# Both MLPs of a two-layer trunk: seven block products for four more groups of the down projection, with shared buffers

## Chip, cores and metric

One core of a Trainium2 chip runs the whole kernel. The metric is the device time of one execution in microseconds; lower is better. Each group of runs is told by its median.

## The reference, cut to what matters

The input is a sequence of 1024 tokens of width 1024. A state-space layer with a gated linear unit (GLU), an MLP, a stick-breaking attention layer and a second MLP follow each other, each added to the residual stream through a gate that depends on a vector `c`. Both MLPs are

```python
h = modulate(rms_norm(x, mlp_norm_g[i]), sh_m, sc_m)
ff = einsum('bsf,fd->bsd', square(relu(einsum('bsd,df->bsf', h, mlp_w1[i]))), mlp_w2[i])
x = x + g_m[:, None, :] * ff
```

with an inner width of 4096. All of it is float32. The gates, shifts and scales (`ada_chunks`) are products of `silu(c)` with matrices of 1024 rows, and the projections of keys, values and queries have a bias that is the product of such a shift with their weights.

## The kernel before

Activations lie transposed: 128 features on the partitions, 512 tokens (a half, `h` = 0 or 1) in a row. A product of two float32 numbers is made of three float32r matmuls (`mm3`, L243): both operands are split into a rounded high part (`uh`, `hi`) and the rest (`ul`, `lo`). The high part is a copy on ScalarE (ACT), the rest a subtraction on VectorE (DVE).

**The MLP** (`mlp`, from L873) has 32 inner tiles in 8 groups `c` of four (`j` = 0 to 3). For an inner tile, `ups` loads one weight unit of 128x1024 (512 KB) into a `raw` buffer through SyncE's queue (SP), splits it, and `up` makes 24 matmuls for each half; ACT takes the relu from PSUM into a buffer `r`, DVE squares it, and `halves` splits it into two tiles of a ring `f`. The down projection of a group has 4 output pairs `op`. *Plain*: for each of 2 outputs and 2 halves, 4 inner tiles times 3 matmuls, so 192 matmuls in a group, and one DVE operation (`down`, L93 in the profile) adds the gated sum to the residual tile. *Seven products*: the 2x2 blocks (2 outputs x 2 halves) are multiplied with seven block products in place of eight, each of 6 matmuls, so 168 in a group. For this `enter` adds and subtracts the hidden blocks (right operands T1 to T4, B11, B21, B22), `blocks` adds and subtracts the weight blocks, the first three of which are split on ACT and DVE and the other four on GpSimd (POOL: four adds of 128x256, a cast and a subtraction of 128x1024), and `seven` gathers the products in two sum tiles `u` and `v`. Before the change `fast(c)` is true for groups 1 to 6 of the second MLP alone.

The order of an MLP is: `ups` of the next group's first inner tile, the down projection of this group, `ups` of the next group's other three tiles. In the last group the plain code goes through the outputs twice, once for each half, and loads each weight unit twice.

**Side work.** During the GLU stage and the first MLP, a list `side` is worked off by `pump`: `mid` takes 3 or 4 jobs after every output pair and every inner tile. Its jobs are of three kinds. A `gemv` (L171) loads 512 KB into a `raw` buffer, the same three buffers that the MLP's weights go through, and DVE multiplies and sums it against a row (`silr` for the gates and shifts, `row` for the biases). A `shift_row` brings a shift into `row` by PE and ACT. A `keep` (L221) prepares half a unit of the attention's weights on POOL: DMA into a buffer `ks`, scale, cast into `kr`, subtract, and two DMAs out (`kh`, `kl`), all issued from POOL's queue. There are 16 `keep` jobs in the GLU stage and 48 in the first MLP.

The order of instructions on each engine is set when the program is built: tiles, pools and waits come from the framework, whose scheduler orders the instructions of all engines; every engine then works in order. A tile of a pool waits until the last reader of the buffer that it takes is done.

Of the kernel before, what the change touches and what calls it, by code (L numbers as in the profile page):

```python
# [30 lines left out]
W2_COLS = (range(8), (0, 1, 2, 3, 6, 7, 4, 5))  # L31
# [25 lines left out]
def kernel(ctx, tc, A, out):  # L57
# [163 lines left out]
    def keep(key, src, c, scale=None):  # L221
# [3 lines left out]
        raw = adap.tile([P, HN], F32, tag="ks", name=nm("ks"), bufs=2)  # L225
# [32 lines left out]
    def s5(hook):  # L258
# [19 lines left out]
        def wide(tag):  # L278
            return un_tile(tag, F32)

# [578 lines left out]
    def open_f(n):  # L859
        fp = ctx_f.enter_context(tc.tile_pool(name="fp", bufs=1))  # L860

        def ft(tag, bufs, dt=F32):
            return fp.tile([P, HN], dt, tag=tag, name=nm(tag), bufs=bufs)

        def f_tile(dt=F32R):
            return ft("f", n, dt)

        return ft, f_tile

    def mlp(layer, xs, hs, norm, fs, mid=None, done=None):  # L870
        w1, w2 = A["w1"][layer], A["w2"][layer]
        gm = M_GM0 if layer == 0 else M_GM1
        ft, f_tile = fs  # L873
        hid, raws = {}, {}

        def up(f, u, h):
# [3 lines left out]
            r = ft("r", 2 + 4 * layer)  # L880
# [10 lines left out]
        def down(c, o, u, i, h):  # L891
            p = ps_ax()
            for j in range(4):
                mm3(p, u, W2_COLS[layer][4 * i + j], hid[j, h], j == 0, j == 3)
# [3 lines left out]
        def enter(j, h, r):  # L898
            raws[j, h] = r
            if h == 0 and j < 2:  # L900
                hid["B11", j] = halves(r)
            if (j, h) == (1, 1):
                for i in range(2):
                    t = ft("t", 2)
                    sub(t, raws[i, 1], raws[i, 0])
                    hid["T1", i] = halves(t)
            if h == 1 and j >= 2:
                i = j - 2
# [3 lines left out]
                sub(b12, b22, b12)  # L912
                hid["T3", i] = halves(b12)
                add(b11, b11, b12)
# [22 lines left out]
        def seven(c):  # L937
            us, sums, op_ = {}, {}, [0]
# [5 lines left out]
            def product(op, n):  # L944
# [10 lines left out]
                op_[0] = op  # L955
                if n == 1:
                    sums[op] = ft("t", 2), ft("t", 2)
                    ACT.copy(sums[op][0], p)
# [4 lines left out]
                elif n == 6:  # L963
                    add(sums[op][0], p, sums[op][0])
                elif n == 5:
                    u, v = sums[op]
                    add(v, p, u)
                    gain(0, 1, v)
                elif n == 7:
                    u, v = sums[op]  # L970
# [7 lines left out]
            for op in range(4):  # L978
                for n in (1, 2, 4, 6, 5, 7, 3):
                    product(op, n)  # L980

        def plain(c, j, h, r):
            raws[j, h] = r
            late = c == 7 and layer == 1
            if not late or h == 0 or j > 1:
                hid[j, h] = halves(r)
            elif j == 1:
                hid[0, 1], hid[1, 1] = halves(raws[0, 1]), halves(r)

        def fast(c):  # L990
            return layer == 1 and 0 < c < 7

        def ups(c, j):
            u = load_unit(w1[4 * c + j])
            for h in range(2):
                r = up(4 * c + j, u, h)
                if fast(c):
                    enter(j, h, r)
                else:
                    plain(c, j, h, r)  # L1000
# [10 lines left out]
        for c in range(8):  # L1011
            if c < 7:
                held = dict(hid)
                hid.clear()
                ups(c + 1, 0)
                nxt = dict(hid)
                hid.clear()
                hid.update(held)
                if fast(c):
                    seven(c)  # L1020
                else:
                    for op in range(4):
                        u = load_unit(w2[c, op])
                        for i in range(2):
                            for h in range(2):
                                down(c, 2 * op + i, u, i, h)
                        if mid is not None:
# [698 lines left out]
```

## Time and profile before

| | us |
|---|---|
| median of 3 runs | 2512.99 (2507.63 to 2521.70) |
| the profiled execution, its own time | 2512.54 |
| span of its profile | 2510.7 |
| TensorE (PE) busy | 2358.1 (94%) |
| VectorE (DVE) busy | 1739.4 (69%) |
| ScalarE (ACT) busy | 939.4 (37%) |
| GpSimd (POOL) busy | 882.1 (35%) |

The stages, in us from the start of the span: the state-space layer to about 250, the GLU to about 405, the first MLP to 1143, attention to about 1800, its output projection to about 1850, the second MLP to the end. PE's matmuls overlap, so that its busy time is no measure of its pace; a count of matmuls over a stretch is. The granted clock of TensorE was 0.973 of full speed over the run.

### The profile page before, as it was taken

The numbers are of one execution on the slowest core, as the hardware profiler recorded it, in microseconds if no ns is written. First come the engines' busy times: TensorE is split into PE (matmuls) and PEld (weight loads), VectorE is DVE, ScalarE is ACT, GpSimd is POOL, SyncE is SP. The second block draws the span as 40 slices with busy tenths as digits, with TensorE's granted clock in tenths as the row PEclk, the third lists the DMA queues.
The fourth block names the chain that finished last, engine by engine and source line by source line (L and its number), as shares of the span: only waits on it lengthen the run. The fifth ranks groups of instructions, "written<-read, shape, count | busy, mean of one in ns | idle before, by whom it ended". The sixth has DMA issues, their size and how long they took to land.

```text
span 2510.7 us, 33266 instructions
## 1 busy us (share of the span) xinstructions
PE 2358.1 (94%) x12560; PEld 1986.0 (79%) x12560; DVE 1739.4 (69%) x2536; ACT 939.4 (37%) x1704; POOL 882.1 (35%) x939
## 2 busy tenths in 40 slices
PE   3888999999999999999899999998999999999999
PEld 2677788878778888888788888887778888888887
DVE  7997547775567553345687878788583777877774
ACT  5753124221121221133566666676351332223221
POOL 4663460376786000013333323343110323342330
PEclk8998999999999999998999999999999999999999
DMA  4225862666767441123111122126621111111113
GB/s 150 87 78 187 297 215 101 237 229 222 248 206 270 154 139 55 51 90 116 64 55 39 64 68 68 58 88 214 246 86 59 34 51 59 59 34 59 51 67 109
DMA packets 105920, 299.18 MB, mean 119 GB/s; under 512 B 13344, under 2 KB 25632, under 8 KB 105760
## 3 DMA queue, kind: packets, MB, share of 16 engines
q1 hardware_dynamic: 87840, 242.52, 28.2%
q0 software_dynamic: 15360, 50.34, 5.7%
q10 hardware_dynamic: 2560, 4.20, 0.7%
q8 instruction: 99, 1.62, 0.3%
q14 instruction: 61, 0.50, 0.1%
HBM read 243.33 MB, written 49.48 MB: 117 GB/s over the span
## 4 chain that ended last, share of the span: by engine, by line
PE 65%; DVE 15%; DMA 10%; issue 4%; ACT 3%; POOL 1%; SPq 0%; DVEq 0%; ACTq 0%; POOLq 0%
PE pm L247 9%; PE pm L249 9%; PE pm L248 9%; PE pm L70 8%; DMA raw<-in_adaT_dram 5%; PE pa L953 3%; PE pa L952 3%; PE pa L954 3%; PE pa L247 3%; PE pa L249 3%; PE pa L248 3%; PE pt L70 3%; DVE sn L1236 3%; PE z L70 2%; PE po L70 2%
## 5 line engine op out<-in xcount | busy, mean ns | idle before, releaser
L247 PE MATMUL pm<-h,uh 128*128 128x512 f32 x1200 | 467.7, 392 | 8.7 <-ACT r L881 8.6
L249 PE MATMUL pm<-h,ul 128*128 128x512 f32 x1200 | 468.7, 392 | 3.1 <-DVE ul L84 3.1
L248 PE MATMUL pm<-h,uh 128*128 128x512 f32 x1200 | 469.5, 391 | 0.0
L214 ACT CAST uh<-raw 128x1024 fp32r<-128x1024 f32 x138 | 145.1, 1051 | 535.2 <-PE pa L248 155.1
L84 DVE TENSOR_TENSOR ul<-raw,uh 128x1024 fp32r<-128x1024 f32 (+1 forms) x162 | 202.5, 1250 | 141.2 <-ACT uh L214 109.4
L247 PEld LDWEIGHTS pm<-h,uh 128*128 128x128 f32 x1200 | 226.8, 189 | 58.7 <-ACT r L881 11.6
L249 PEld LDWEIGHTS pm<-h,ul 128*128 128x128 f32 x1200 | 226.4, 189 | 51.9 <-DVE ul L84 4.5
L248 PEld LDWEIGHTS pm<-h,uh 128*128 128x128 f32 x1200 | 226.7, 189 | 47.9 <-DVE h L93 0.9
L174 DVE CUSTOM_DVE_ANT_0 junk<-raw,silr 128x1024 bf16<-128x1024 f32 x95 | 133.2, 1402 | 142.3 <-DMA raw<-in_adaT_dram 142.2
L70 PE MATMUL pm<-uh,h 128*128 128x256 f32 x960 | 225.5, 301 | 4.1 <-POOL h L75 3.0
L1236 DVE TENSOR_TENSOR_SCAN sn<-sn 128x768 f32<-128x768 f32 (+7 forms) x128 | 180.4, 1415 | 48.8 <-ACT sn L1231 47.5
L887 ACT CAST f<-r 128x512 fp32r<-128x512 f32 x152 | 94.3, 621 | 253.7 <-DVE r L78 216.7
L247 PE MATMUL pa<-f,uh 128*128 128x512 f32 x464 | 181.9, 392 | 3.3 <-DVE xall L93 2.7
L248 PE MATMUL pa<-f,uh 128*128 128x512 f32 x464 | 181.4, 391 | 0.2 <-DVE f L84 0.2
L249 PE MATMUL pa<-f,ul 128*128 128x512 f32 x464 | 181.1, 390 | 0.0
L70 PEld LDWEIGHTS pm<-uh,h 128*128 128x128 f32 x960 | 170.2, 197 | 6.2 <-POOL h L75 3.2
L81 POOL TENSOR_TENSOR acc<-acc,sq 128x512 f32<-128x512 f32 x24 | 34.7, 1445 | 351.8 <-ACT sq L819 351.7
L84 DVE TENSOR_TENSOR f<-r,f 128x512 fp32r<-128x512 f32 x152 | 124.4, 820 | 45.2 <-ACT f L887 43.9
L81 POOL TENSOR_TENSOR raw<-raw 128x256 f32<-128x256 f32 x24 | 22.3, 931 | 377.8 <-DVE ul L84 377.8
L93 DVE SCALAR_TENSOR_TENSOR x<-pa,mod,x 128x512 f32<-128x512 f32 x143 | 103.4, 743 | 61.9 <-PE pa L249 59.8
L70 PE MATMUL pm<-ul,h 128*128 128x256 f32 x480 | 138.4, 288 | 0.0
L78 DVE TENSOR_TENSOR r<-r 128x512 f32<-128x512 f32 (+1 forms) x130 | 97.0, 746 | 57.6 <-ACT r L881 57.6
(371 smaller groups left out, 5471.0 us busy)
## 6 DMA issues: line engine op xcount, KB each, us to landing
raw<-in_w_dram SPq DMA_DIRECT2D x144, 512.0 KB, 3.3
raw<-in_adaT_dram SPq DMA_DIRECT2D x96, 512.0 KB, 4.0
uh<-kh SPq DMA_DIRECT2D x40, 512.0 KB, 4.0
ul<-kl SPq DMA_DIRECT2D x40, 512.0 KB, 4.1
kh<-kr POOLq DMA_DIRECT2D x64, 256.0 KB, 2.6
kl<-ks POOLq DMA_DIRECT2D x64, 256.0 KB, 3.7
raw<-in_wT_dram SPq DMA_DIRECT2D x24, 512.0 KB, 4.2
raw<-in_wglu_dram SPq DMA_DIRECT2D x20, 512.0 KB, 4.5
```

Of the source, the lines that this page charges most:

```text
L70: return lambda *a, **k: tc.keep_in_program_order(f(*a, **k))
L78: eng.tensor_tensor(o, a, b, op=ALU.mult)
L84: eng.tensor_tensor(o, a, b, op=ALU.subtract)
L93: V.scalar_tensor_tensor(o, a, s, b, op0=op0, op1=op1)
L174: V.tensor_tensor_reduce(junk, raw, row, 1.0, 0.0, op0=ALU.mult, op1=ALU.add, accum_out=bcol)
L214: ACT.copy(uh, raw)
L247: T.matmul(ps, uh[:, sl], hi, start=first, stop=False)
L248: T.matmul(ps, uh[:, sl], lo, start=False, stop=False)
L249: T.matmul(ps, ul[:, sl], hi, start=False, stop=last)
L887: ACT.copy(hi, r)
L952: T.matmul(p, uh[:, sl], hi, start=(i == 0), stop=False)
L1236: V.tensor_tensor_scan(g[:, s0:], g[:, s0:], g[:, s0:], 1.0, op0=ALU.mult, op1=ALU.bypass)
```

## The change

- `fast` is true for groups 4, 5 and 6 of the first MLP and for 1 to 7 of the second. The columns of `w2` are ordered in the same way for both layers.
- The hidden tiles of both MLPs are now one ring of 28 (`Inner`; before 20 and 30), which the norm's tiles share. The squares have two buffers `ra` for `j` < 2 and two `rb` for `j` >= 2 (before: 2 buffers `r` in the first MLP, 6 in the second); `u` and `v` take the two `rb` buffers. The inner tiles of a group are made in the order 0, 2, 1, 3.
- In group 7 of the second MLP all four results of an output pair are written out after it.
- To make room: `ks` has one buffer (before 2), `gemv` writes its product over `raw` in place of `junk`, and `row` is gone: `shift_row` writes over `silr`. For that the side list has all `gemv` jobs with `silr` first, then the first `shift_row` with 16 bias jobs, then the second with 8. The numbers of jobs are the same. Later pools have 3 `raw` buffers in place of 2.

```diff
-        pools["raw"] = es.enter_context(tc.tile_pool(name=f"raw{i}", bufs=3 - i))
+        pools["raw"] = es.enter_context(tc.tile_pool(name=f"raw{i}", bufs=3))
...
-        V.tensor_tensor_reduce(junk, raw, row, 1.0, 0.0, op0=ALU.mult, op1=ALU.add, accum_out=bcol)
+        V.tensor_tensor_reduce(raw, raw, row, 1.0, 0.0, op0=ALU.mult, op1=ALU.add, accum_out=bcol)
...
-        raw = adap.tile([P, HN], F32, tag="ks", name=nm("ks"), bufs=2)
+        raw = adap.tile([P, HN], F32, tag="ks", name=nm("ks"), bufs=1)
...
+    class Inner:
+        def __init__(self):
+            self.n, self.es, self.pools = 0, ExitStack(), {}
+        def open(self, name):
+            self.pools[name] = self.es.enter_context(tc.tile_pool(name="fp" + name, bufs=1))
+        def tile(self, dt=F32R):
+            a = self.n % 28 < 8
+            self.n += 1
+            return self.pools["ab"[not a]].tile([P, HN], dt, tag="f", name=nm("f"), bufs=8 if a else 20)
+        def raw(self, tag):
+            return self.pools["b"].tile([P, HN], F32, tag=tag, name=nm(tag), bufs=2)
...
-            r = ft("r", 2 + 4 * layer)
+            r = fs.raw(tag)
...
         def fast(c):
-            return layer == 1 and 0 < c < 7
+            return c in ((4, 5, 6), range(1, 8))[layer]
...
+                if c == 7:
+                    for k in range(2 * op, 2 * op + 2):
+                        for h in range(2):
+                            done(k, h)
...
+                for j in (2, 1, 3):
+                    ups(c + 1, j)
...
-    queue(ada_chunk(M_KSH) + [lambda: shift_row(M_KSH)] + bias_jobs(0, 16)
-          + ada_chunk(M_SHA1) + [lambda: shift_row(M_SHA1)] + bias_jobs(16, 24) + [kq_gain]
-          + ada_chunk(M_GA1) + ada_chunk(M_SHM1)
-          + ada_chunk(M_SCM1, lambda: scale_cols(3, M_SCM1)) + ada_chunk(M_GM1), 2,
+    queue(ada_chunk(M_KSH) + ada_chunk(M_SHA1) + ada_chunk(M_GA1) + ada_chunk(M_SHM1)
+          + ada_chunk(M_SCM1, lambda: scale_cols(3, M_SCM1)) + ada_chunk(M_GM1)
+          + [lambda: shift_row(M_KSH)] + bias_jobs(0, 16)
+          + [lambda: shift_row(M_SHA1)] + bias_jobs(16, 24) + [kq_gain], 2,
```

Three places of the built program show what this moves. The first is POOL while `keep` jobs run in the first MLP, before: the load into the second `ks` buffer (here `ks_5672`) is issued ahead of the subtraction of the first.

```order
L232 CAST kr_5589<-ks_5588 128x512
L227 DMA ks_5672<-in_wkv_dram 128x512
L84 TENSOR_TENSOR ks_5588<-ks_5588,kr_5589 128x512
L235 DMA kh_5586<-kr_5589 128x512
L235 DMA kl_5587<-ks_5588 128x512
L78 TENSOR_TENSOR ks_5672<-ks_5672,scl 128x512
```

The same engine in the changed program, where the 45th of all 64 `keep` jobs meets the first weight blocks of group 4 (`raw_6556`): the load of the next `ks` stands behind the DMA out of this one, and the blocks' cast and subtraction stand behind that load.

```order
L81 TENSOR_TENSOR raw_6556<-raw_6556 128x256
L84 TENSOR_TENSOR ks_6747<-ks_6747,kr_6748 128x512
L235 DMA kh_6745<-kr_6748 128x512
L84 TENSOR_TENSOR raw_6556<-raw_6556 128x256
L235 DMA kl_6746<-ks_6747 128x512
L84 TENSOR_TENSOR raw_6556<-raw_6556 128x256 x2
L227 DMA ks_6836<-in_wkv_dram 128x512
L947 CAST uh_6560<-raw_6556 128x1024
L78 TENSOR_TENSOR ks_6836<-ks_6836,scl 128x512
L84 TENSOR_TENSOR ul_6561<-raw_6556,uh_6560 128x1024
```

A load now waits for its predecessor's `kl`, and four more instructions of a block stand between a `keep` job's own. The third place is DVE in the down projection of group 4. Before, `gemv` jobs (the ISA rows) stand between the gated sums (`xall`):

```order
L93 SCALAR_TENSOR_TENSOR xall<-pa_6598,mod,xall 128x512
L174 ISA junk,mod<-raw_6967,silr 128x1024
L174 ISA mod 128x1
L93 SCALAR_TENSOR_TENSOR xall<-pv_6612,mod,xall 128x512
L174 ISA junk,mod<-raw_6978,silr 128x1024
L174 ISA mod 128x1
```

In the changed program the bias jobs of the first `shift_row` stand between the products' sums (`rb_6554` and `rb_6555` are `u` and `v`); there are 15 of them in this down projection, and 8 in that of group 5:

```order
L174 ISA raw_6653,bias<-raw_6653,silr 128x1024
L174 ISA bias 128x1
L174 ISA raw_6739,bias<-raw_6739,silr 128x1024
L174 ISA bias 128x1
L93 SCALAR_TENSOR_TENSOR xall<-pv_6678,mod,xall 128x512
L93 SCALAR_TENSOR_TENSOR xall<-pa_6687,mod,xall 128x512
L93 SCALAR_TENSOR_TENSOR xall<-pa_6695,mod,xall 128x512
L174 ISA raw_6742,bias<-raw_6742,silr 128x1024
L174 ISA bias 128x1
L81 TENSOR_TENSOR rb_6554<-pv_6703,rb_6554 128x512
```

The sums of a product are thus queued behind loads of 512 KB. Before, such bias jobs stood in the down projections and inner tiles of groups 1 to 3.

## Rows read from the trace of the kernel before

**Rows 1.** The page, part 1: busy us (share of the span) and instructions.

```profile
PE 2358.1 (94%) x12560; PEld 1986.0 (79%) x12560; DVE 1739.4 (69%) x2536; ACT 939.4 (37%) x1704; POOL 882.1 (35%) x939
```

**Rows 2.** Stretches: length, PE busy (count), PEld, DVE, ACT, POOL, clock, DMA, GB/s.

```profile
465.00:848.00 383.00, 365.35 (x1578) 297.66 (x1577) 247.55 (x294) 70.44 (x100) 252.51 (x286) 0.98 0.67 230
848.00:1020.00 172.00, 172.00 (x761) 142.41 (x760) 84.20 (x119) 35.45 (x50) 0.00 (x0) 1.00 0.30 101
1960.00:2440.00 480.00, 480.00 (x2119) 397.61 (x2118) 375.12 (x485) 133.39 (x199) 169.99 (x144) 1.00 0.15 52
```

**Rows 3.** Timeline of ACT: the relu before groups 0's and 4's down projections.

```profile
464.73 0.59 ACT L881 ACTIVATE r<-pm 128x512 f32<-128x512 f32 x1
...
848.11 0.59 ACT L881 ACTIVATE r<-pm 128x512 f32<-128x512 f32 x1
```

**Rows 4.** Waits of PE, 400 to 1150: total us, times, longest.

```profile
PE pm L247 <- ACT r L881: 7.6, 5, 2.6
```

**Rows 5.** Groups by shape, DVE, 600 to 810: busy us, mean ns, idle before.

```profile
L174 DVE CUSTOM_DVE_ANT_0 junk<-raw,row 128x1024 bf16<-128x1024 f32 x20 | 30.6, 1528 | 16.0 <-DMA raw<-in_wT_dram 15.3 <-ACT row L1523 0.6
...
L84 DVE TENSOR_TENSOR f<-r,f 128x512 fp32r<-128x512 f32 x16 | 17.3, 1081 | 6.2 <-ACT f L887 6.2
L78 DVE TENSOR_TENSOR r<-r 128x512 f32<-128x512 f32 x16 | 15.5, 971 | 5.8 <-ACT r L881 5.8
```

**Rows 6.** Groups by shape, DVE, 1960 to 2440.

```profile
L93 DVE SCALAR_TENSOR_TENSOR x<-pa,mod,x 128x512 f32<-128x512 f32 x96 | 68.8, 741 | 2.0
L93 DVE SCALAR_TENSOR_TENSOR x<-t,mod,x 128x512 f32<-128x512 f32 x72 | 66.5, 944 | 0.8
L81 DVE TENSOR_TENSOR t<-pa,t 128x512 f32<-128x512 f32 x96 | 63.8, 684 | 21.2 <-PE pa L954 21.1
...
L84 DVE TENSOR_TENSOR r<-r,r 128x512 f32<-128x512 f32 x24 | 31.4, 1310 | 0.4
```

**Rows 7.** Groups by shape, POOL, 468 to 810: one `keep` job's compute.

```profile
L84 POOL TENSOR_TENSOR ks<-ks,kr 128x512 f32<-128x512 f32 x48 | 67.5, 1407 | 1.5
L78 POOL TENSOR_TENSOR ks<-ks,scl 128x512 f32<-128x512 f32 x48 | 65.1, 1358 | 125.3 <-DVE scl L93 71.5 <-DMA ks<-in_wkv_dram 38.4 <-DMA ks<-in_wq_dram 14.9
L232 POOL CAST kr<-ks 128x512 fp32r<-128x512 f32 x48 | 44.9, 936 | 15.4 <-DMA kh<-kr 13.6
```

**Rows 8.** DMA issues, 600 to 720, then 840 to 960: KB, median us to landing.

```profile
raw<-in_wT_dram SPq DMA_DIRECT2D x12, 512.0 KB, 4.4
...
kl<-ks POOLq DMA_DIRECT2D x16, 256.0 KB, 3.7
...
ks<-in_wkv_dram POOLq DMA_DIRECT2D x13, 256.0 KB, 3.4
...
raw<-in_w_dram SPq DMA_DIRECT2D x13, 512.0 KB, 3.4
```

**Rows 9.** Timeline of POOL: start, us, what, idle before it and its releaser.

```profile
468.71 3.40 POOL L78 TENSOR_TENSOR ks<-ks,scl 128x512 f32<-128x512 f32 x2 [71.55 <-DVE scl L93]
...
638.89 0.54 POOL L235 DMA_DIRECT2D kl<-ks  x1
...
642.26 0.54 POOL L227 DMA_DIRECT2D ks<-in_wkv_dram  x1 [0.84 <-DMA kl<-ks]
...
646.77 1.20 POOL L78 TENSOR_TENSOR ks<-ks,scl 128x512 f32<-128x512 f32 x1 [1.64 <-DMA ks<-in_wkv_dram]
```

**Rows 10.** Groups by shape, POOL, 1960 to 2440: one `blocks` call has 1, 3, 1, 1.

```profile
L84 POOL TENSOR_TENSOR ul<-raw,uh 128x1024 fp32r<-128x1024 f32 x24 | 63.5, 2646 | 1.9
L84 POOL TENSOR_TENSOR raw<-raw 128x256 f32<-128x256 f32 x72 | 59.2, 822 | 5.6
L930 POOL CAST uh<-raw 128x1024 fp32r<-128x1024 f32 x24 | 25.0, 1041 | 29.3 <-PE pm L248 28.2
L81 POOL TENSOR_TENSOR raw<-raw 128x256 f32<-128x256 f32 x24 | 22.3, 931 | 377.8 <-DVE ul L84 377.8
```

**Rows 11.** Timeline at the end of the span: the last DVE operation.

```profile
2506.24 0.75 DVE L93 SCALAR_TENSOR_TENSOR x<-pa,mod,x 128x512 f32<-128x512 f32 x1 [1.97 <-PE pa L249]
```

More of the change, by code (lines that the diff above doesn't have):

```diff
@@ L30 @@
 LEAD = 24
-W2_COLS = (range(8), (0, 1, 2, 3, 6, 7, 4, 5))
+W2_COLS = (0, 1, 2, 3, 6, 7, 4, 5)
 NONE = 3
@@ L279, in wide @@
             return un_tile(tag, F32)
+        row = st([P, D], "row")
         braw = wide("uh").rearrange("p (l q h) -> p l q h", l=2, q=32)
@@ L872, in mlp, with up @@
         gm = M_GM0 if layer == 0 else M_GM1
-        ft, f_tile = fs
+        f_tile = fs.tile
         hid, raws = {}, {}
-        def up(f, u, h):
+        def up(f, u, h, tag="ra"):
             p = ps_mm()
@@ L899, in enter @@
             raws[j, h] = r
[L900 to L906, printed above, removed]
+            i = j % 2
+            if (j, h) == (1, 0) or (j, h) == (2, 0):
+                hid["B11", i] = halves(raws[i, 0])
             if h == 1 and j >= 2:
-                i = j - 2
                 b11, b12, b21, b22 = raws[i, 0], raws[i, 1], raws[j, 0], raws[j, 1]
@@ L937, in seven @@
         def seven(c):
-            us, sums, op_ = {}, {}, [0]
+            us, op_, uv = {}, [0], (fs.raw("rb"), fs.raw("rb"))
             def gain(i, h, src):
@@ L955, in product @@
                 op_[0] = op
+                u, v = uv
                 if n == 1:
-                    sums[op] = ft("t", 2), ft("t", 2)
-                    ACT.copy(sums[op][0], p)
+                    ACT.copy(u, p)
                 if n < 3:
@@ L963, in product @@
                 elif n == 6:
[L964 removed]
+                    add(u, p, u)
                 elif n == 5:
[L966 removed]
                     add(v, p, u)
@@ L980, in seven @@
                     product(op, n)
+                if mid is not None:
+                    mid()
+                if c == 7:
+                    for k in range(2 * op, 2 * op + 2):
+                        for h in range(2):
+                            done(k, h)
         def plain(c, j, h, r):
             raws[j, h] = r
[L984 to L988, printed above, removed]
+            if c and j == 0:
+                return
+            if c and (j, h) == (2, 0):
+                hid[0, 0], hid[0, 1] = halves(raws[0, 0]), halves(raws[0, 1])
+            hid[j, h] = halves(r)
         def fast(c):
-            return layer == 1 and 0 < c < 7
+            return c in ((4, 5, 6), range(1, 8))[layer]
         def ups(c, j):
@@ L1012, in mlp @@
             if c < 7:
-                held = dict(hid)
-                hid.clear()
                 ups(c + 1, 0)
[L1016 to L1027, printed above, removed]
-                            mid()
-                hid.clear()
-                hid.update(nxt)
-                for j in range(1, 4):
-                    ups(c + 1, j)
+            if fast(c):
+                seven(c)
+            elif c < 7:
+                for op in range(4):
+                    u = load_unit(w2[c, op])
+                    for i in range(2):
+                        for h in range(2):
+                            down(c, 2 * op + i, u, i, h)
                     if mid is not None:
@@ L1041, in mlp @@
                             done(2 * op + i, h)
+            if c < 7:
+                for j in (2, 1, 3):
+                    ups(c + 1, j)
+                    if mid is not None:
+                        mid()
     def attention(xn, bias, xd):
@@ L1444 @@
     silr = rowp.tile([P, D], F32, name="silr")
-    junk = rowp.tile([P, D], BF16, name="junk")
-    row = rowp.tile([P, D], F32, name="row")
     def gate(i):
@@ L1522, in shift_row @@
                          start=True, stop=True)
-            ACT.copy(row[:, HN * h:HN * h + HN], p)
+            ACT.copy(silr[:, HN * h:HN * h + HN], p)
     def kq_gain():
@@ L1701, in _layout @@
     a["w2"] = np.stack([w.reshape(8, 4, 128, 4, 2, 128).transpose(0, 3, 2, 4, 1, 5).reshape(8, 4, 128, 8, 128)[
-        :, :, :, list(cols)].reshape(8, 4, 128, 1024) for w, cols in zip(mlp_w2, W2_COLS)])
+        :, :, :, list(W2_COLS)].reshape(8, 4, 128, 1024) for w in mlp_w2])
     return {k: np.ascontiguousarray(v) for k, v in a.items()}
```

64 lines of the change are left out of this document (31 added, 33 removed).

## The prediction

> **What bounds the kernel now.** I read the page first, then the stretches of both MLPs, then who waits there, and last the queues that the change touches. The page has PE at 94% of the span [rows 1], but that is a mean. What is to be seen in the stretches is the count of matmuls. In the second MLP PE starts 2119 in 480 us, one every 0.2265 us, at full clock; in groups 4 and 5 of the first it starts 761 in 172 us, the same pace [rows 2]. There PE alone sets the time, and each matmul that goes is worth 0.2265 us. Between the relus ahead of the down projections of groups 0 and 4 [rows 3], 465 to 848, it starts 1578, for which that pace needs 357 us; the stretch takes 383, so about 26 us are lost there. Its other columns tell why: POOL is busy 252 us in it and not at all in the next stretch, and the DMAs move 230 GB/s against 101 [rows 2]. POOL's `keep` jobs run there beside the `gemv` loads. PE waits among others for a relu that has no free buffer `r` [rows 4].
>
> **The matmuls removed.** Four groups have 168 in place of 192: 4 x 24 x 0.2265 = **21.7 us less**, if PE stays the bound in all of them.
>
> **Groups 0 to 3 of the first MLP.** Their own matmuls don't change, but three things around them do. The bias jobs, bunched behind the first `shift_row` in groups 1 and 2, move to groups 4 and 5; four buffers stand where two held the squares, so that the wait of rows 4 should shrink; and `keep` jobs come at a slower rate (next part), which takes traffic from the `raw` loads. A 512 KB load lands in 4.4 us while they run and in 3.4 us without them [rows 8]. Nothing of the 26 us may come back, or all of it; I take half: **14 us less** (0 to 26).
>
> **POOL with one `ks` buffer.** Now one job after the other: load 3.4 us [rows 8], scale 1.36, cast 0.94, subtraction 1.41 [rows 7], the issue of `kh` 0.56, and `kl` 3.7 us to landing [rows 8], together 11.4 us. Single rows are near it: `kl` issued at 638.89 lets the next load go at 642.26, 3.4 us later, but that load holds the scaling up until 646.77, 4.5 us later [rows 9]; with 4.5 a job takes 12.5. The first scaling starts at 468.7 [rows 9], and the 45th job, with which the first blocks of group 4 stand, is 28 jobs later: 468.7 + 28 x 11.4 = 788, and the blocks are ready about 17 us after that (rest of both jobs 7, the wait for `kl` and the load 7, `ul` 2.65 [rows 10]), at 805. PE needs them with its 19th matmul there, 4 us into that down projection, which starts at 465 + 348 (four groups of 384 matmuls) + 12 (what I leave of the loss) = 825. So the jobs are 24 us early and hidden; that cover is gone when a job takes 12.2 us. Inside groups 4 to 6 one call of `blocks` takes 0.93 + 3 x 0.82 + 1.04 + 2.65 = 7.1 us [rows 10] and has about one job around it, whose two waits for DMAs now stand in front of the blocks' cast and subtraction: some 14 us for each output pair, where PE takes 9.5. The built order lets PE run ahead with the high parts and with 18 matmuls of the next inner tile, so little of it is left: **4 us more** (0 to 30).
>
> Of this the Trainium skill says two things. "Trainium Kernel Development and Optimization", Best Practices, asks for double buffers so that DMAs lie beside compute, which speaks against this edit; by that rule the rival below with the slow `keep` chain is the case. "DMA: Bandwidth & Descriptors", Anatomy of one DMA, gives about 2.0 us and the bytes at 436 GB/s for a DMA from POOL's queue, 2.6 us for 256 KB; the rows show 3.4 and 3.7, so the trace doesn't agree, and I go by the rows. By the page a job would take 9.5 us and the 4 us would fall away.
>
> **DVE in groups 4 and 5.** The products of one down projection give it 16 gated sums from PSUM at 0.741, 12 from `u` or `v` at 0.944 and 16 additions at 0.684 [rows 6], 34 us; with the 15 bias jobs of group 4 at 1.53 us [rows 5], 23 us, and four splits of weights it has some 64 us, while PE would be through in 168 x 0.2265 = 38. It can catch up in the next 192 matmuls of inner tiles (43.5 us), where it has 14 splits at 1.08, 8 squares at 0.97 [rows 5] and 8 additions at 1.31 at most [rows 6], 33 us. All these are lengths from stretches in which POOL runs, as it will there. With two more splits of weights that is 99 us against PE's 81.5, 17.5 too much if every operation takes its whole row and nothing lies beside a wait that PE has anyway; the buffers of `u` and `v`, which the next relus wait for, pass it on to PE. At the other end nothing: DVE had 84 us of work in 172 in these groups and PE lost none [rows 2]. I take **12 us more in group 4** (0 to 24), nearer to the upper end, since the bias jobs stand bunched in its first half. Group 5 has 8 bias jobs, 10 us less work: **4 more** (0 to 13). Group 6 has none: **1 more**, for the two buffers `ra`, whose release now waits for the end of a chain of six splits and four additions that takes about as long as the 10.9 us that PE gives it.
>
> **Group 7 of the second MLP.** Before, its last half ran at PE's pace to the end, where one operation of 0.75 us was left [rows 11]. Now the right operands of the last inner tile are made when PE has no further inner tile to do: ten DVE operations and a square, some 9 us, against 30 matmuls that don't need them, 6.8 us: **3 more**. And behind the last product stand two additions, of which most lies under PE, and three gated sums (0.74 + 2 x 0.94), each of which is written out after it: **2.5 more**. The halved weight loads there cost nothing before (PE kept its pace), and gain nothing.
>
> **The rest** I cost at nothing: `gemv` writing a float32 result over `raw`, which no row shows (it reads the same, so nothing; at most the length of two squares, 1.94 us for 1.53 [rows 5], 6 us over the 15 in group 4, which with the 17.5 is its upper end), the third `raw` buffer of the second MLP (PE keeps its pace there without it [rows 2]), and the slower `keep` jobs of the GLU stage, 10.0 us each without the scaling, about one for each 10.9 us of PE (48 matmuls).
>
> **Sum**, against the profiled execution's own 2512.5 us, half a microsecond below the median of 2513.0: 2512.5 - 21.7 - 14 + 4 + 12 + 4 + 1 + 3 + 2.5 = 2503.3; I say **2504 us**. The nearest thing to know is that the largest terms, 14 and 12, are both half of their ranges.
>
> **Rivals.**
> *The stalls go and DVE copes* (2490 us). All 26 us come back and of the 21 us of stalls in groups 4 to 6 two thirds stay: 2512.5 - 21.7 - 26 + 14 + 5.5 = 2484 at best; with 20 of the 26 it is 2490. For it: in groups 4 and 5 PE lost nothing beside the loads that were left [rows 2]. Against it: `keep` jobs go on, and DVE's sums are added.
> *DVE is the bound and nothing comes back* (2518 us): the forecast without the 14 us. For it: the side list pumps as many jobs per group as before. Against it: the bunch behind `shift_row` leaves groups 1 and 2.
> *The `keep` chain becomes the bound* (2530 us), the one that ends on the other side. If one job takes 12.5 us, as the single rows say, the first blocks of group 4 are ready at 468.7 + 28 x 12.5 + 17 = 836, 7 us after PE wants them, and each of groups 4 to 6 needs six to seven jobs more, 7 us each: 28 us in place of 4 is 2528, and what waits behind POOL adds a little. It decides from 12.2 us a job on. For it: the loads in the rows that waited are slower than the median. Against it: with half the rate of jobs the DMAs should land sooner.
> That the change doesn't do what it says is no rival: 98 rows fewer stand in PE's order.
>
> **Chances.** A measurement of this kernel can tell about 0.5%, 12.5 us, from no change; the forecast lies 9 us below, inside it. Forecast, 2504 with 2494 to 2514 around it: 0.42, of which 0.26 is within 0.5% and 0.16 faster. Stalls gone: 0.22, faster. DVE bound: 0.14, of which 0.08 within and 0.06 slower. `keep` chain: 0.22, of which 0.02 within and 0.20 slower. Together faster 0.38, within 0.5% 0.36, slower 0.26. The range reaches from 2484 to 2534, which leaves out the best of the second case and the worst of the last.
>
> **What would show it.** Right, step by step: 96 matmuls fewer at 0.2265 us where PE runs dense; 465 to the down projection of group 4 in about 360 us in place of 383, with a shorter PE wait for relus; `keep` jobs 11 to 12 us apart and ended near 1080 in place of 808; group 4 longer than 87 us, DVE near full in it, the bias jobs between 825 and 960; group 7 of the second MLP ending 3.4 us after its last matmul. Wrong: if PE waits in group 4 for POOL's `ul`, it is the `keep` chain; if groups 0 to 3 still lose over 20 us, the loads and not the bunch were the cause; if DVE has idle time in group 4 while PE has none, the 12 us were never there.

## The result, and the profile after

The changed kernel takes 2539.03 us (median of 4 runs, 2534.53 to 2545.92) where the kernel before, run beside it, takes 2510.31 (2505.63 to 2521.70): a ratio of 1.0108, with an interval of 1.0086 to 1.0131. It is slower by 1.1%, and the time lies above the forecast's range. The profiled execution took 2538.69 us.

The page after, the span and the busy times, against [rows 1]: PE has its 96 matmuls less, DVE 98 us and POOL 114 us more.

```profile
span 2536.5 us, 33439 instructions
## 1 busy us (share of the span) xinstructions
PE 2348.6 (93%) x12464; PEld 1968.8 (78%) x12464; DVE 1837.8 (72%) x2700; ACT 956.2 (38%) x1740; POOL 996.1 (39%) x1035
```

The stretches after, cut at the relus ahead of the down projections: groups 0 to 3, then groups 4, 5 and 6 of the first MLP (columns as in [rows 2]).

```profile
469.12:825.08 355.96, 350.35 (x1540) 288.06 (x1539) 225.05 (x296) 70.70 (x101) 161.34 (x182) 1.00 0.56 194
825.08:937.97 112.89, 92.27 (x373) 73.24 (x372) 92.09 (x116) 23.66 (x37) 69.16 (x64) 0.89 0.48 163
937.97:1043.14 105.17, 91.90 (x376) 72.35 (x376) 82.05 (x99) 23.90 (x38) 63.00 (x62) 0.92 0.37 128
1043.14:1122.84 79.70, 74.20 (x319) 58.77 (x318) 55.26 (x65) 17.85 (x27) 49.70 (x52) 1.00 0.30 109
```

Groups 0 to 3 take 356.0 us in place of 383.4, which is 27.4 less. Groups 4 and 5 took 172 us together [rows 2] and now take 218. Cut in the same way, by the relus of before, group 4 took 84.9, group 5 87.0 and group 6 76.2 us: 28.0, 18.2 and 3.5 more, though each has 24 matmuls less. The rest is small: 4.4 us ahead of group 0 (of which 3.2 ahead of the first relu), 3.4 less from the first MLP's last relu to the second MLP's first, 0.1 in the second MLP up to its last relu, and 2.4 behind that. The sum is 25.8 us, the difference of the spans. A little of the 27.4 has only moved behind the relu: the stretch held 1545 matmuls of 512 columns and 32 short ones of the two `shift_row` jobs (4.2 us together), and now holds 1538 of 512 columns and none of the short ones. So about 22 us of stalls went there.

The *down stretches* of groups 4, 5 and 6 after, each from the relu ahead of a down projection to the next relu:

```profile
825.08:901.48 76.40, 56.44 (x223) 43.93 (x221) 64.83 (x80) 9.45 (x13) 49.71 (x46) 0.87 0.54 183
937.97:1006.17 68.20, 54.93 (x213) 41.74 (x213) 56.31 (x68) 9.45 (x15) 44.13 (x44) 0.87 0.43 150
1043.14:1096.04 52.90, 47.40 (x200) 36.60 (x199) 42.72 (x52) 8.91 (x13) 39.07 (x41) 1.00 0.29 106
```

In group 4 PE idles 20 of the 76.4 us and is busy 56.4; its 205 matmuls of 512 columns need 46.4 us at 0.2265 us each and the 16 short ones some 2, so about 8 us more go to matmuls at the lower clock (last section). What PE waits for there:

```profile
PE pv L969 <- DVE xall L93: 6.5, 2, 4.1
PE pm L249 <- DVE ul L84: 5.3, 1, 5.3
PE pa L969 <- POOL uh L947: 3.1, 1, 3.1
PE pa L970 <- DVE f L84: 1.2, 1, 1.2
```

DVE and POOL are both late there. The longest waits behind these stand on SP's queue, in the same stretch, and on POOL (timeline; the last column is the idle time ahead and its releaser):

```profile
SPq L173 <- DVE bias L174: 47.1, 9, 16.6
...
SPq L938 <- DVE bias L174: 3.3, 2, 2.5
```

```profile
841.12 0.54 POOL L235 DMA_DIRECT2D kl<-ks  x1
850.64 0.74 POOL L81 TENSOR_TENSOR raw<-raw 128x256 f32<-128x256 f32 x1 [8.98 <-DVE ul L84]
```

The loop can be read here: a bias job waits on DVE behind the products' sums and holds a `raw` buffer; SP can issue the load of the next weight block only at 842.86; ACT casts it at 848.74 and DVE splits it at 849.60; POOL, idle for 9 us, starts on it at 850.64; and PE waits 3.1 us, up to 857.08, for POOL's cast.

The `keep` jobs go nearly at the pace forecast: the first scaling in the first MLP at 473.1, the 45th at 809.88, so 12.0 us a job (forecast 11.4), the last at 1109.3. POOL had the first blocks of group 4 ready at 824.4 (forecast 805), just ahead of that down projection.

```profile
L78 POOL TENSOR_TENSOR ks<-ks,scl x48: 1034/1138/2137, 473.1 to 1109.3; 128x512 f32<-128x512 f32 x48
```

The end of the program (timeline; compare [rows 11]): the last matmul starts at 2529.83, and two additions and three gated sums of DVE go on to 2533.1, as forecast.

```profile
2529.83 0.39 PE L971 MATMUL pa<-f,ul 128*128 128x512 f32 x1
2529.84 1.28 DVE L81 TENSOR_TENSOR rb<-pa,rb 128x512 f32<-128x512 f32 x2
2531.04 0.74 DVE L93 SCALAR_TENSOR_TENSOR x<-pa,mod,x 128x512 f32<-128x512 f32 x1
2531.69 1.41 DVE L93 SCALAR_TENSOR_TENSOR x<-rb,mod,x 128x512 f32<-128x512 f32 x2
```

### The profile page after: what moved, and what is told of

Read it like the earlier page. It is cut to its first block, busy times and chain, and to the rows that moved or that the text cites. A ratio compares the mean times of both kernels' runs of the same rounds, so it can differ in the third digit from the quotient of the medians.

```text
span 2536.5 us, 33439 instructions
## 1 busy us (share of the span) xinstructions
PE 2348.6 (93%) x12464; PEld 1968.8 (78%) x12464; DVE 1837.8 (72%) x2700; ACT 956.2 (38%) x1740; POOL 996.1 (39%) x1035
## 4 chain that ended last, share of the span: by engine, by line
PE 61%; DVE 20%; DMA 10%; issue 4%; ACT 2%; POOL 1%; SPq 0%; DVEq 0%; ACTq 0%; POOLq 0%
PE pm L70 8%; PE pm L249 8%; PE pm L247 8%; PE pm L248 8%; DMA raw<-in_adaT_dram 6%; PE pa L971 4%; PE pa L969 4%; PE pa L970 4%; PE pt L70 3%; DVE xall L93 3%; DVE sn L1250 3%; DVE raw L174 2%; PE z L70 2%; PE po L70 2%; PE pa L249 2%
## 5 line engine op out<-in xcount | busy, mean ns | idle before, releaser
L247 PE MATMUL pm<-h,uh 128*128 128x512 f32 x1200 | 468.3, 393 | 12.9 <-ACT rb L901 9.4
L248 PE MATMUL pm<-h,uh 128*128 128x512 f32 x1200 | 469.7, 391 | 0.9 <-DVE h L93 0.9
L214 ACT CAST uh<-raw 128x1024 fp32r<-128x1024 f32 x118 | 123.9, 1050 | 427.9 <-PE pa L248 127.9
L174 DVE CUSTOM_DVE_ANT_0 raw<-raw,silr 128x1024 f32<-128x1024 f32 x119 | 162.7, 1369 | 164.2 <-DMA raw<-in_adaT_dram 153.8
L84 DVE TENSOR_TENSOR ul<-raw,uh 128x1024 fp32r<-128x1024 f32 (+1 forms) x158 | 190.7, 1208 | 94.0 <-ACT uh L214 69.2
L81 POOL TENSOR_TENSOR raw<-raw 128x256 f32<-128x256 f32 x40 | 38.0, 951 | 463.0 <-DVE ul L84 458.3
L1250 DVE TENSOR_TENSOR_SCAN sn<-sn 128x768 f32<-128x768 f32 (+7 forms) x128 | 179.4, 1407 | 48.5 <-ACT sn L1245 47.3
L969 PE MATMUL pa<-f,uh 128*128 128x512 f32 x500 | 199.9, 400 | 12.8 <-POOL uh L947 6.9
L970 PE MATMUL pa<-f,uh 128*128 128x512 f32 x500 | 197.9, 396 | 1.2 <-DVE f L84 1.2
L971 PE MATMUL pa<-f,ul 128*128 128x512 f32 x500 | 187.4, 394 | 0.1
L78 POOL TENSOR_TENSOR sg<-sg,sn 128x512 f32<-128x512 f32 x64 | 92.9, 1452 | 120.7 <-DVE sn L1250 51.9
L93 DVE SCALAR_TENSOR_TENSOR x<-pa,mod,x 128x512 f32<-128x512 f32 x143 | 103.6, 743 | 41.5 <-PE pa L249 34.7
L78 POOL TENSOR_TENSOR ks<-ks,scl 128x512 f32<-128x512 f32 x48 | 61.3, 1278 | 177.0 <-DMA ks<-in_wkv_dram 101.1
L1245 ACT ACTIVATE sn<-z,rrr 128x512 f32<-128x512 f32 (+1 forms) x192 | 111.6, 581 | 47.5 <-PE z L70 45.8
L70 PE MATMUL pm<-h,uh 128*128 128x512 f32 x386 | 128.7, 415 | 0.0
```

The lines of the kernel that those rows point to most:

```text
L70: return lambda *a, **k: tc.keep_in_program_order(f(*a, **k))
L78: eng.tensor_tensor(o, a, b, op=ALU.mult)
L84: eng.tensor_tensor(o, a, b, op=ALU.subtract)
L93: V.scalar_tensor_tensor(o, a, s, b, op0=op0, op1=op1)
L174: V.tensor_tensor_reduce(raw, raw, row, 1.0, 0.0, op0=ALU.mult, op1=ALU.add, accum_out=bcol)
L247: T.matmul(ps, uh[:, sl], hi, start=first, stop=False)
```

## The experiments

Theory A: the bias jobs on DVE, bunched between the products' sums, are the loss. Theory B: besides them POOL, which has weight blocks and `keep` jobs in one queue. Theory C: the products cost it by themselves. A down stretch is as above. Ratios are to the kernel before on the same chip, which takes 2517 to 2518 us there; the times expected were reckoned from 2510, so compare ratios.

| | ratio (95% interval) | down stretch of group 4, 5, 6, us |
|---|---|---|
| the change | 1.0108 [1.0086, 1.0131] | 76.4, 68.2, 52.9 |
| e1 no bias jobs | 0.9991 [0.9978, 1.0005] | 52.7, 54.7, 55.3 |
| e2 first MLP plain | 0.9975 [0.9954, 0.9995] | 52.3, 49.8, 47.3 |
| e3 products in group 6 alone of the first | 1.0015 [0.9999, 1.0032] | 50.1, 49.8, 55.1 |
| e4 side jobs in the inner tiles | 1.0095 [1.0078, 1.0112] | 57.4, 64.9, 58.8 |
| e5 no late `keep` jobs | 0.9955 [0.9939, 0.9972] | 57.4, 53.4, 43.2 |
| e6 neither | 0.9880 [0.9864, 0.9897] | 45.0, 45.1, 43.2 |
| e7 before, one `ks` | 0.9928 [0.9906, 0.9949] | 44.7, 40.9, 47.3 |
| e8 before, bias jobs late | 0.9996 [0.9984, 1.0009] | 49.8, 49.8, 47.3 |
| e9 before, `keep` loads on SP | 0.9969 [0.9951, 0.9987] | 44.8, 43.5, 47.3 |
| e10 e9 with one `ks` | 0.9992 [0.9979, 1.0005] | 45.8, 40.6, 47.3 |
| e11 e2 with group 7 of the second plain | 0.9970 [0.9954, 0.9987] | 51.5, 49.8, 47.3 |
| e12 the change, `keep` loads on SP | 1.0142 [1.0119, 1.0166] | 73.9, 64.7, 52.4 |

**e1, without the bias jobs** (the bias of keys, values and queries is left at zero).

```diff
+    G.memset(bias, 0.0)
-        return [(lambda i=i: gemv(A["wT"][i], silr, bias[:, i:i + 1])) for i in range(lo, hi)]
+        return [(lambda: None) for i in range(lo, hi)]
```

> The changed kernel without the 24 bias jobs (no load, no DVE product; the bias is set to zero once), everything else as it is. Theory A (the bias jobs, bunched behind the two shift_row calls, stand between the products' sums on DVE and make the down projections of groups 4 and 5 as long as DVE's queue): group 4 falls from 112 us to about 88, group 5 from 105 to about 88, group 6 stays at 80, and the time falls by about 40 us, to 2498. Rival B (POOL: the single ks buffer delays the weight blocks): nothing of that kind is taken away, groups 4 and 5 stay above 100 us, 2530 or more. Rival C (the block products themselves are too much for DVE and POOL in the first MLP): less than half comes back, 2520 to 2530.

2515.94 us. Groups 4 and 5 fall from 113 and 105 us to 92 and 91, so the bias jobs are a good part of the loss. But it is not the 2498 us of theory A, and all three down stretches stay at 53 to 55 us. The timeline of POOL in group 5 shows what is left: the casts of three blocks come 14.7 and 13.7 us apart, with a `keep` job between them.

```profile
931.27 1.39 POOL L947 CAST uh<-raw 128x1024 fp32r<-128x1024 f32 x1
932.97 1.55 POOL L78 TENSOR_TENSOR ks<-ks,scl 128x512 f32<-128x512 f32 x1 [0.31 <-DMA ks<-in_wq_dram]
...
945.43 0.56 POOL L227 DMA_DIRECT2D ks<-in_wq_dram  x1 [1.51 <-DMA kl<-ks]
945.99 1.05 POOL L947 CAST uh<-raw 128x1024 fp32r<-128x1024 f32 x1
948.31 1.04 POOL L78 TENSOR_TENSOR ks<-ks,scl 128x512 f32<-128x512 f32 x1 [1.26 <-DMA ks<-in_wq_dram]
...
959.73 1.05 POOL L947 CAST uh<-raw 128x1024 fp32r<-128x1024 f32 x1
```

Between two casts POOL computes for about 11 us, issues three DMAs in 1.7 us and waits for DMAs 1.8 and 1.3 us. In e6 (below), where PE never idles, the same casts come 11.45 us apart. So POOL's own work and issues, without any wait, are already longer than PE's step.

**e2, plain down projections in the first MLP; e3, products in its group 6 alone.**

```diff
-            return c in ((4, 5, 6), range(1, 8))[layer]
+            return c in ((), range(1, 8))[layer]
```

for e2, and for e3

```diff
+            return c in ((6,), range(1, 8))[layer]
```

> The changed kernel with no group of the first MLP on seven products; the second MLP, the buffers and the order of the side jobs stay. Theory A: the bias jobs now stand between 16 plain sums a group, where DVE has room: groups 4 to 6 take 87 us each, as before the change, and the 27 us that groups 0 to 3 gained stay: 2510 - 27 + 4 (start of the first MLP) - 1 = 2486, range 2482 to 2495. Rival B: the keep jobs feed no block here, the same 2486, so it doesn't tell A from B, but if the jobs on POOL cost PE in another way, groups 4 to 6 stay above 90 us each and the time above 2500.

> The changed kernel with group 6 alone of the first MLP on seven products, where no bias job is left but keep jobs go on. Theory A: 5.4 us less than with none if DVE copes, 2481; the 9 us that group 6 lost in the changed kernel beside its own matmuls were DVE's lag from group 5. Rival B: the 9 us were POOL's, they stay, and the time is 2486 to 2491, no better than with none.

2511.43 and 2521.43 us: e3's expectation, 2481 by theory A, falls and its rival B (the loss is POOL's, no better than with none) stands, and e2 misses its 2486 too: groups 0 to 3 gave back 20 us in place of 27, and groups 4 to 6, with the bias jobs in them, take 259 us in place of 248. Group 6 costs more with products than without even where groups 4 and 5 are plain and hand it no arrears: 81.9 us against 76.2. With products in no group of the first MLP the ratio is 0.9975, in one 1.0015, in three 1.0108: each group that is added loses. Part of the difference to the figures expected is not in the MLP at all: in both runs and in e11, and in no other, PE halts 13.8 us at the start of attention (why the built order halts there was not tried); from the first MLP's last relu to the second's first is 761.5 and 763.4 us, against 755.0 before. In e2's timeline:

```profile
1167.44 0.77 PE L247 MATMUL pm<-h,uh 128*128 128x512 f32 x1 [13.83 <-issue]
```

**e4, side jobs of groups 4 to 6 pumped twice after each of the three inner tiles that follow a down projection, and not in the down projection.**

```diff
-                if mid is not None:
-                    mid()
...
                     if mid is not None:
                         mid()
+                        if fast(c):
+                            mid()
```

> The changed kernel with the side jobs of groups 4 to 6 pumped after the inner tiles alone, two pumps for each, and none between the products. Theory A: the bias jobs leave the down projection for the inner tiles, where DVE has some 10 us of room a group: a good part of the 55 us of groups 4 and 5 comes back, 2505 to 2520. Rival B: keep jobs and blocks are still on POOL one behind the other, above 2530. Rival C: as the changed kernel, above 2530.

2539.45 us, no gain. The jobs are queued in the inner tiles but spill over: POOL is busy 40, 45 and 39 us in the three down stretches, where the blocks alone take 20 (e6 below), and DVE 48, 54 and 45. A place in the program is not a time on an engine that is behind.

**e5, without the last 20 `keep` jobs; e6, without these and without the bias jobs.** With the change and e1 they make a square.

```diff
+        if key[0] == "q" or key[:2] == ("kv", 7):
+            kept[key] = kept["kv", 0, 0]
+            return
         if c == 0:
```

> The changed kernel without the last 20 keep jobs (all of the queries' weights and those of the last pair of heads), which in the changed kernel run beside groups 4 to 6 of the first MLP; the attention layer reads the prepared weights of the first pair in their place. The bias jobs stay. Theory A (the bunched bias jobs on DVE are the whole loss of groups 4 and 5): the down projections of groups 4 and 5 stay near 76 and 68 us, about 2530 us. Theory B (bias jobs on DVE, and besides them POOL, which makes blocks and keep jobs in one queue, some 14 us for each output pair where PE takes 9.5): what the run without bias jobs still lost goes too, 10 to 12 us in each of the three down projections: about 64, 56 and 43 us, 2539 - 35 = 2505 us. Theory C (the products' sums on DVE cost this much in the first MLP by themselves): as A.

> The changed kernel without the 24 bias jobs and without the same 20 keep jobs: nothing but the products is left beside PE in groups 4 to 6 of the first MLP. The run without the bias jobs alone had down projections of 53, 55 and 55 us there and 2516 us. Theory B (POOL is what is left): 43 to 45 us each, as in the second MLP, 2516 - 33 = 2483 us. Theory C (the products cost it by themselves): still 52 to 55 us, 2514 us.

2505.72 and 2487.82 us: theory B, whose figures were 2505 and 2483. A and C fall. The three down stretches, first e1, then e5, then e6:

```profile
832.38:885.08 52.70, 48.40 (x211) 39.05 (x210) 42.37 (x52) 9.25 (x14) 38.07 (x37) 0.97 0.28 96
924.16:978.86 54.70, 49.00 (x207) 37.83 (x206) 43.56 (x53) 9.47 (x13) 39.16 (x38) 0.97 0.32 106
1015.45:1070.75 55.30, 49.11 (x198) 37.12 (x197) 44.30 (x52) 8.91 (x13) 39.69 (x42) 0.97 0.30 105
```

```profile
831.00:888.40 57.40, 52.21 (x229) 42.37 (x227) 55.08 (x77) 9.48 (x14) 24.98 (x18) 0.97 0.48 157
924.80:978.20 53.40, 48.55 (x207) 39.23 (x206) 50.60 (x68) 9.47 (x14) 24.31 (x18) 0.94 0.41 134
1015.90:1059.10 43.20, 43.20 (x192) 35.81 (x191) 39.64 (x53) 8.86 (x13) 20.27 (x18) 1.00 0.18 61
```

```profile
830.97:875.97 45.00, 45.00 (x208) 37.56 (x207) 41.06 (x52) 9.47 (x14) 19.92 (x18) 1.00 0.17 59
914.39:959.49 45.10, 45.10 (x209) 37.63 (x208) 41.09 (x52) 9.52 (x15) 19.93 (x18) 1.00 0.18 59
997.81:1041.01 43.20, 43.20 (x192) 35.81 (x191) 39.67 (x53) 8.84 (x13) 20.28 (x18) 1.00 0.18 61
```

With neither, PE has no idle time at all, and the down stretches are close to the 43.2 us of the second MLP; the 1.9 us more in groups 4 and 5 are the short matmuls of the two `shift_row` jobs. Over the three groups the bias jobs alone cost 154.0 - 133.3 = 20.7 us, the `keep` jobs alone 162.7 - 133.3 = 29.4, both together 197.5 - 133.3 = 64.2: 14 us more than the sum. (The stretches do not hold quite the same matmuls. With each of 512 columns taken off at 0.2265 us, and the 16 short ones of a `shift_row` at 2 us, the three costs are 16, 28 and 58 us, and again 14 over the sum.) Removing a `keep` job takes away its work on POOL, its traffic and what it does to DVE at once. The traffic is hardly the cost: a weight load lands in 3.3 to 3.9 us (medians) in the three down stretches of e1 and in 3.2 to 3.3 in those of e6.

One reason for the 14 us can be read on DVE: with the `keep` jobs on POOL, the same operations take longer. In the down stretch of group 5 DVE's 68 instructions take 50.6 us in e5 and 56.3 in the change. Lines by shape, of one group each with and without `keep` jobs: the split of a weight unit in group 6 (e1, then e6) and the bias job in group 4 (the change, then e5).

```profile
L84 DVE TENSOR_TENSOR ul<-raw,uh 128x1024 fp32r<-128x1024 f32 x3 | 5.0, 1691 | 0.0
```

```profile
L84 DVE TENSOR_TENSOR ul<-raw,uh 128x1024 fp32r<-128x1024 f32 x3 | 3.6, 1212 | 0.0
```

```profile
L174 DVE CUSTOM_DVE_ANT_0 raw<-raw,silr 128x1024 f32<-128x1024 f32 x13 | 20.0, 1553 | 5.4 <-DMA raw<-in_wT_dram 5.4
```

```profile
L174 DVE CUSTOM_DVE_ANT_0 raw<-raw,silr 128x1024 f32<-128x1024 f32 x13 | 16.8, 1298 | 0.0
```

It does not hold for every operation in every group. DVE's second pass over `u` and `v` (L93, both inputs in SBUF) takes 1288 ns in group 4 of the change against 1071 in e5, but 1090 in e1 against 1102 in e6. So POOL's share alone does not set it; what does was not followed up. The other reason is the loop through the `raw` buffers above. How the 14 us divide between the two was not tried; a run with a fourth `raw` buffer could tell.

**e12, the change with the `keep` loads issued by SP.**

```diff
-        G.dma_start(raw, src[:, cs])
+        SP.dma_start(raw, src[:, cs])
```

> The changed kernel with the loads of keep jobs issued by SP. In POOL's queue the wait for such a load stood between the casts and subtractions of the blocks; it goes, the work of POOL stays but for 0.55 us of issue a job. Theory B1 (the waits for DMAs in POOL's queue make the 14 us per output pair): 11 us per pair, each of the three down projections 8 us shorter, 2515 us, ratio 1.001. Theory B2 (POOL's own work and what it takes from DVE): 13 us or more per pair, 2532 to 2540 us, ratio 1.008 to 1.011.

2552.35 us. The down stretches hardly move (73.9, 64.7, 52.4). But the edit takes only a part of the waits away, so it does not decide between B1 and B2: in the three down stretches POOL waits 11.7, 6.5 and 3.4 us for DMAs of `keep` jobs, against 10.7, 12.1 and 6.6 in the change, and in group 5 a wait of 6.5 us for a load still stands between a block's cast (998.99) and its subtraction (1008.36). Where waits went, in groups 5 and 6, 5.6 and 3.2 us of them, the stretches are 3.5 and 0.5 us shorter. For B2 speaks the timeline of e1 above: of the 14 us per pair POOL's waits for DMAs are under 2. The loss against the change is elsewhere: groups 0 to 3 take 372.9 us in place of 356.0, since SP now waits for the one `ks` with the weights' loads behind it. That was not expected.

**e7, the kernel before with one `ks` buffer; e8, the kernel before with the side list in the new order.** These ask what shortened groups 0 to 3.

```diff
-        raw = adap.tile([P, HN], F32, tag="ks", name=nm("ks"), bufs=2)
+        raw = adap.tile([P, HN], F32, tag="ks", name=nm("ks"), bufs=1)
```

This is e7. e8 keeps `row` and both buffers and takes over the three lines of the side list from the diff of the change.

> The kernel before with one ks buffer in place of two, nothing else. The keep jobs come about 12 us apart in place of about 8 and reach into groups 4 to 6, whose down projections are plain. Theory B1 (a keep job is hidden wherever POOL makes no blocks, and what it costs is the traffic and the shared SBUF access, which move with it): groups 0 to 3 some 10 us shorter, groups 4 to 6 some 10 us longer, 2505 to 2515 us. Rival (one buffer costs by itself, as the skipped overlap of load and store would say): 10 us or more longer, 2523 us.

> The kernel before with the side list in the order of the changed kernel (all jobs with silr first, then both shift_rows with their bias jobs), the separate row and two ks buffers kept. If the bias jobs bunched behind the first shift_row made group 1 of the first MLP long (107 us against 89 to 96 for its neighbours), that goes: 2511 - 15 = 2496 us, and groups 4 and 5, plain there, take the bias jobs at no cost. If the pace of the keep jobs and their traffic made it long, nothing changes: 2508 to 2514 us.

2502.31 and 2518.17 us. Groups 0 to 3 in e7, in e8, and in e9 (below):

```profile
470.77:835.75 364.98, 356.35 (x1581) 293.33 (x1580) 222.98 (x294) 71.34 (x101) 156.41 (x179) 1.00 0.61 203
```

```profile
469.33:850.29 380.96, 354.01 (x1530) 287.72 (x1529) 248.02 (x285) 67.96 (x97) 251.96 (x286) 0.99 0.66 222
```

```profile
467.93:849.08 381.15, 362.71 (x1581) 297.30 (x1580) 238.31 (x294) 71.22 (x101) 222.82 (x240) 0.98 0.68 232
```

The bunch behind `shift_row` was not the cause of the whole: moved away, it gives 2 us of 383. It did make group 1 long, which falls from 107 to 94 us, but with other `gemv` jobs in its place group 0 grows from 96 to 105 and group 2 from 89 to 100. One buffer gives 18. The jobs are then 12 us apart and reach to 1029 us in place of 802, so POOL works 156 us beside groups 0 to 3 in place of 252 [rows 2]. DVE has the same 294 instructions there and needs 223 us in place of 248; the split of a square takes 764 ns in place of 1130 (before, then e7, lines by shape over groups 0 to 3):

```profile
L84 DVE TENSOR_TENSOR f<-r,f 128x512 fp32r<-128x512 f32 x31 | 35.0, 1130 | 14.0 <-ACT f L887 13.9
```

```profile
L84 DVE TENSOR_TENSOR f<-r,f 128x512 fp32r<-128x512 f32 x31 | 23.7, 764 | 13.8 <-ACT f L887 13.7
```

Groups 4 to 6, which now have the other `keep` jobs beside plain down projections, take 249.3 us against 248.1 before: hidden, where some 10 us were expected, so that the time is below the expected one. So one buffer in place of two makes the kernel before 0.7% faster; of the kernels that leave nothing out this is the fastest of the study. That the gain comes by DVE's shorter operations is argued from these rows; the DMA traffic beside groups 0 to 3 fell as well, from 230 to 203 GB/s.

**e9 and e10, the kernel before with the `keep` loads on SP, with two buffers and with one** (the edit of e12, and for e10 that of e7).

> The kernel before, two ks buffers kept; the load of a keep job is issued by SP, in order with the weights' loads, in place of POOL. POOL can then not run ahead of the MLP: a job starts when SP comes to its load. Theory P (what one ks buffer gave back in the kernel before is the pace: jobs spread over seven groups in place of four): the last job ends after 950 us in place of 808, groups 0 to 3 of the first MLP take 360 to 368 us in place of 383, ratio to before 0.989 to 0.996. Rival (the buffer itself matters, or SP's queue is held up by waits for a ks): groups 0 to 3 at 380 us or more, ratio 0.999 to 1.01.

> The same with one ks buffer. Theory P: the same pace from another cause, ratio 0.989 to 0.996, no better than with two buffers. Rival: SP waits for the one buffer with weight loads behind it, ratio over 1.0.

2507.61 and 2516.10 us. e9 does not do what it was made for: the last job still starts at 824 us, the loads being issued early enough, and groups 0 to 3 stay at 381 us. Not spread, no gain there: that fits theory P, but it is no proof of it; why its median is 0.3% under the kernel before is open (its profiled span is no shorter). e10 spreads the jobs to 1028 us and groups 0 to 3 take 373.3 us, but SP, waiting for the one buffer, gives the rest back, group 4 taking 100 us against 84.9. The pace helps only where nothing else queues behind the wait that makes it.

**e11, e2 with group 7 of the second MLP plain** (`range(1, 7)` for the second layer).

> The changed kernel with plain down projections in the whole first MLP and in group 7 of the second; against the run that had them plain in the first MLP alone it shows what group 7 is worth. From the last relu to the end of the span the runs with seven products in group 7 took 47.6 to 49.2 us, those with a plain one 45.9 to 46.3: 2 us less, ratio to before 0.9965 (0.9975 for that run). Rival (as forecast, 5.4 gained and 5.5 lost): the same 48 us, ratio 0.9975.

2508.20 us. From the last relu to the end of the span it takes 46.0 us against 47.7 in e2, as 46.3 before and 48.7 in the change: products in group 7 lose about 2 us. The intervals of the two ratios overlap, so the times alone do not show it.

## Why the prediction was wrong, step by step

*The matmuls removed* (21.7): counted rightly, and paid back where nothing is late: group 6 of e6 takes 71.6 us, 4.6 of the 5.4 less than the 76.2 before.

*Groups 0 to 3* (14 less, 0 to 26): 27.4 less, of which about 5 are matmuls that now lie behind the relu (7 of 512 columns, 1.6 us, and the short ones of `shift_row`, about 4), so some 22 us of stalls, within the bound. The prediction's 1578 counts the 32 short matmuls like the others, so that the loss before was nearer to 30 us than to 26. The cause named first, the bunch of bias jobs, does not carry it (e8); the slower rate of the `keep` jobs, named third, gives 18 (e7). The 4 us that are left are within scatter: seven kernels with the change's buffers and its side jobs in groups 0 to 3 (e1 to e6, e11) take 358.0 to 365.8 us there, and the change's 356.0 is the lowest.

*POOL with one `ks` buffer* (4 more, 0 to 30): **this step failed.** Its parts were nearly right: 12.0 us a job, the first blocks of group 4 in time, some 14 us of POOL for each output pair. What failed is the sentence "The built order lets PE run ahead with the high parts and with 18 matmuls of the next inner tile, so little of it is left". Such a lead, 18 matmuls or 4.1 us, is spent once; the arrears come at every output pair. PE's step is not the 9.5 us of the products alone but, with the inner tile's matmuls that the built order puts among them, 11.45 (e6), against POOL's 13.7 and 14.7 (e1). So the `keep` jobs cost 29 us without the bias jobs, 7.7, 9.6 and 12.1 in the three down stretches: about the 28 us of the third rival, and the end of this term's own bound. But that rival was tied to a job of over 12.2 us; the pace of one job decided nothing, the sum of jobs and blocks in one queue did. So that the rival's time is nearer than the forecast's is in part luck. The sign that the prediction gave for it, a wait of PE for POOL's `ul`, does not show in group 4 either: of PE's waits there one, of 3.1 us, is for POOL's cast, and the rest are for DVE. The rule of the Trainium skill that the prediction weighed ("Trainium Kernel Development and Optimization", Best Practices: double buffers) is not borne out by e7, where a single buffer is 0.7% faster: there PE never waits for a `keep` job. The change with two `ks` buffers was not run.

*DVE in groups 4 to 6* (12 + 4 + 1 = 17): alone it was sized well. DVE has 64.8 us of work in the down stretch of group 4 (80 instructions; forecast 64), and the bias jobs alone cost 12.4, 8.3 and 0 us (e5 against e6; over the whole groups 10.4, 7.7 and 0). **What failed here** is that the terms of DVE and POOL were added, and what one does to the other was put at nothing: together they cost another 14 us. The bias jobs kept the length of [rows 5] (1553 against 1528 ns; POOL is busy 74% of the time there and 65% in group 4 after). The second pass over `u` and `v` did not keep that of [rows 6], 1288 against 944 ns: POOL is busy 35% of that stretch.

*Group 7 of the second MLP* (5.4 less, 5.5 more): 2.4 more in place of 0.1. The end behind the last matmul is as forecast; the 2.3 us beyond the forecast are two waits of PE for the casts of right operands (`f`, ACT), which before, in the same place, do not occur.

*The rest.* `gemv` over `raw` costs nothing (1553 ns against the 1528 of [rows 5]). The 4.4 us ahead of group 0 were not costed; at least part is scatter, as e8, which does the same as the kernel before up to there, has its first relu 3.6 us later too.

In one line: against the forecast groups 0 to 3 are 13 us better, groups 4 to 6 45 us worse (+49.7 for +4.7; about 5 us of both are the matmuls that moved from one to the other), the second MLP 2 us worse, and the rest is 1 us. By whole groups the 45 are: the `keep` jobs 27 in place of 4, the bias jobs 18 in place of 17, both together 14 more in place of nothing, and the matmuls removed 9.7 in place of 16.3 (e6), mostly by those that moved.

## What to carry to other kernels

Where a helper engine has a job to do in every step of a loop, compare its whole time for one step, with everything else in its queue, to the time the main engine takes for that step; a lead at the start covers the difference once, not in each step. Two suspects that use the same engines and buffers are to be removed one at a time and together, since their costs need not add. And a background job that nobody waits for can be too fast: spread over seven groups in place of four, one cost 18 us less.

## What was not expected of the hardware

DVE operations with two inputs in SBUF can grow with what POOL does at the time: the split of a weight unit takes 1212 ns without `keep` jobs and 1691 with them (group 6 of e6 and e1), that of a square 764 and 1130 (e7 and before), while the gated sums from PSUM stay at 738 to 743 in all of these runs. The Trainium skill ("SBUF — State Buffer", SBUF: two separate sides) says that such a DVE operation and a GpSimd operation that reads SBUF take a shared pair of ports from each other for a whole instruction each; these rows agree. The prediction, which took such lengths as fixed, did not draw on it.

A stall also took clock: the granted clock of TensorE, 1.00 in the down stretches of e6, was 0.87 in those of groups 4 and 5 of the change. The timeline of PE in group 4 shows how: after a wait of 2.35 us the matmuls first start 0.23 us apart, and from 844.89 on 0.43 apart, which is the pace of the lower of the two levels (1.2 of 2.4 GHz), up to 847.87.

```profile
843.55 0.50 PE L969 MATMUL pv<-f,uh 128*128 128x512 f32 x1 [2.35 <-DVE xall L93]
...
844.89 0.63 PE L971 MATMUL pv<-f,ul 128*128 128x512 f32 x1
845.31 0.63 PE L971 MATMUL pa<-f,ul 128*128 128x512 f32 x1
```
